# A hybrid encoder layer on one core: the short convolution in token order, and RWKV's output weights and merge operands by pairs of columns

## The chip, the cores and the metric

The kernel runs on one core of one Trainium2 chip. The metric is the device time of one execution in microseconds (us); the median over several runs is compared. The engines of a core are named PE (matrix multiply, with PEld for its weight loads), DVE (vector), ACT (scalar and activation), POOL and SP (which here issues the DMA transfers). Each works through its own list of instructions in a fixed order and waits at an instruction until what it needs is there.

## The reference

One layer of an encoder, for 1024 tokens of 1024 channels in float32:

```python
x = x + 0.5 * swiglu(rmsnorm(x, ffn1_norm), ffn1_w_gu, ffn1_w_down)
h = rmsnorm(x, mix_norm)
u_hy, u_rw, g_hy, g_rw = split(h @ w_in)          # 1536, 1952, 1024, 1024 columns
uc = w[0] * u_hy[t-1] + w[1] * u_hy[t] + w[2] * u_hy[t+1] + b    # centred width-3 conv
x1, x2, v = split(uc)                             # 512 channels each
z = x1 * long_conv(v, k_f[:, 0]); z = x2 * long_conv(z, k_f[:, 1])
y_hy = z @ hy_out
y_rw = rwkv7_two_scans(u_rw) @ rw_out             # 512 -> 1024 columns
merged = sigmoid(g_hy) * y_hy + sigmoid(g_rw) * y_rw
x = x + merged @ w_out
x = x + 0.5 * swiglu(rmsnorm(x, ffn2_norm), ffn2_w_gu, ffn2_w_down)
out = rmsnorm(x, final_norm)
```

The filters of the long convolution are made in the kernel from positions, by a small network. The time mixing of RWKV is a linear recurrence over the tokens, forward and backward, followed by a group norm, a bonus term and a gate.

## The kernel before

The activations lie transposed, channels on the 128 partitions and tokens along the free dimension. Nearly every large product is made of three products of 128x512 in a reduced float32: a factor is split into a high part and a rest, and hi x hi, lo x hi and hi x lo are summed in PSUM (`mm3`, lines 43 to 45; with the order pinned by `InOrder`, line 55). The split of weights is a cast on ACT (line 33) and a subtraction on DVE or POOL (line 37); `col_weights` loads 128 columns of a weight matrix to `w_st` (line 170, two buffers) and splits them to `w_hi` and `w_lo` (three buffers each).

The stages follow one another: first feed-forward, mixer input, RWKV's scan with other work filled in between, mixer output, second feed-forward. A scheduler lays out the order of each engine before the run, by priority in program order and by its own estimates of when buffers and operands are ready; on the chip the order is then fixed. Instructions that went through `InOrder` keep their order on PE.

Two places matter here.

**Short convolution** (`ShortConv`, within `mixer_in`). Twelve column groups of 128 channels pass through it. Each half of 512 tokens comes from PE in PSUM (`pw`). `take` copies it to `sh_u` (line 545) and writes the middle tap with its bias to `sh_o` (line 546). `finish` adds the two outer taps, each in one DVE pass over 1024 tokens (line 552), transposes eight blocks of 128x128 on PE (line 558, with `sh_o` as the stationary operand and the identity as the moving one), copies the result out on ACT (line 559) and stores it to `d_X` (line 560). Tokens are numbered t = 8 m + r. The long convolution wants, for each r, a block of 128 tokens m by channels. Before, `sh_o` has the shape (r, m): writes to it go in steps of 128 elements, and each transposed block is packed. In the same stage run the filters of the long convolution (lines 420 to 525), on PE, ACT, DVE and POOL.

**Mixer output** (`mixer_out`). The last RWKV blocks still need `RwkvPost`, the norm and gate: a unit `rest` already begun, and two units of blocks 0 and 7 whose operands (`rp_k`, `rp_r`, `rp_y`, `rp_v`, `rp_g`, `rp_gd`) `post.load` fetches. Their results go to `d_yo`, and the second half of the tokens is fetched from there (`z_st`, split to `s_hi` and `s_lo` by `split_half`). Meanwhile the first half can be multiplied with `rw_out`: for each half t and each of eight column groups j, twelve matmuls to `mo_ps` (four PSUM buffers), then on DVE the gate times the product (line 1605), plus Hyena's part (line 1606), and the split to `m_hi` and `m_lo`. The gate `mo_sg` and Hyena's part `mo_mh` are fetched by pairs of column groups, two buffers each (line 1583); the weights by single groups. After both halves comes the product with `w_out`.

## Time and profile before

| | |
|---|---|
| median of 3 runs | 2882.93 us (2874.61 to 2890.05) |
| profiled execution | 2875.99 us, span of its instructions 2874.2 us, mean granted PE clock 0.97 |
| PE busy | 2723.9 us (95%), weight loads 2194.6 us beside it |
| DVE, ACT, POOL busy | 1231.8, 905.2, 550.0 us |
| moved by DMA | 276.43 MB, 96 GB/s in the mean |
| short convolution with filters | from 790 to 1066 us of the span |
| RWKV's output weights | from 1932.8 to 2017.4 us |

The span runs from the first to the last instruction of the profiled execution; its time is a little longer. A page shows how long each engine was busy, then its busy share in 40 slices. A view of waits names for each engine's instruction what released it, and for how long the engine had been idle ahead of it: total, number, longest. A timeline row has start, length, engine, line, operation and, in brackets, the idle time before it and its releaser. A row of a tile gives the shortest, the median and the longest duration in nanoseconds.

### The profile page before, as it was taken

To read this page: it belongs to the slowest core of one execution; us is meant where nothing else is said; L and a number is where in the kernel's file an instruction comes from. 1 tells how busy PE (TensorE), PEld (TensorE's weight loads), DVE (VectorE), ACT (ScalarE), POOL (GpSimd) and SP (SyncE) were. 2 spreads that over 40 slices of the span, in tenths; PEclk is the share of its full clock that TensorE was granted. 3 is DMA by queue.
4 is the path that set the end of the run, shared out by engine and by line. 5 is a ranking of instruction groups with operands and counts; after the bars stand their busy time and mean duration, and the time that the engine had idled before them with its cause. 6 is when DMAs were issued, how large, how long until landed. Compare 5 with 4: busy or idle time off the path is not lost. (4 is left out here: it accounts for less than half of the span.)

```text
span 2874.2 us, 46016 instructions
## 1 busy us (share of the span) xinstructions
PE 2723.9 (95%) x19440; PEld 2194.6 (76%) x19440; DVE 1231.8 (43%) x2140; ACT 905.2 (31%) x1515; POOL 550.0 (19%) x351
## 2 busy tenths in 40 slices
PE   8999999999988899989899999898999999999998
PEld 6888888888665667777787877776778888888787
DVE  4111010111647668998765667757541111101114
ACT  5111111111444442334654545532331111111112
POOL 2323233232413210000000000000033232322322
PEclk9999999999988999999999999898999999999999
DMA  5111111111341235553644325457531111111102
GB/s 126 55 48 48 41 55 48 41 52 43 107 148 63 77 127 186 164 169 114 188 118 152 103 88 180 144 171 231 166 88 52 44 52 44 52 44 48 47 27 92
DMA packets 406477, 276.43 MB, mean 96 GB/s; under 512 B 50899, under 2 KB 366879, under 8 KB 405632
## 3 DMA queue, kind: packets, MB, share of 16 engines
q1 hardware_dynamic: 406272, 273.50, 31.5%
q8 instruction: 153, 2.51, 0.4%
q14 instruction: 52, 0.43, 0.0%
HBM read 202.53 MB, written 70.91 MB: 95 GB/s over the span
## 5 line engine op out<-in xcount | busy, mean ns | idle before, releaser
L45 PE MATMUL pw<-hThi,w_lo 128*128 128x512 f32 (+1 forms) x1184 | 472.3, 400 | 15.6 <-DVE w_lo L1246 15.6
L43 PE MATMUL pw<-hThi,w_hi 128*128 128x512 f32 (+1 forms) x1184 | 473.8, 400 | 8.5 <-ACT sh_o L1268 4.4
L44 PE MATMUL pw<-hTlo,w_hi 128*128 128x512 f32 (+1 forms) x1184 | 472.1, 399 | 0.0
L33 ACT CAST w_hi<-w_st 128x1024 fp32r<-128x1024 f32 (+1 forms) x176 | 170.8, 972 | 496.0 <-PE pw L44 187.0
L37 POOL TENSOR_TENSOR w_lo<-w_st,w_hi 128x1024 fp32r<-128x1024 f32 x100 | 240.5, 2405 | 412.3 <-ACT w_hi L33 406.1
L43 PE MATMUL pgu<-hThi,w_hi 128*128 128x512 f32 x704 | 279.0, 396 | 0.8 <-issue 0.8
L44 PE MATMUL pgu<-hTlo,w_hi 128*128 128x512 f32 x704 | 279.1, 396 | 0.2 <-POOL hTlo L37 0.2
L45 PE MATMUL pgu<-hThi,w_lo 128*128 128x512 f32 x704 | 279.1, 397 | 0.0
L43 PE MATMUL pdn<-g_hi,wd_hi 128*128 128x512 f32 x704 | 275.0, 391 | 1.9 <-DVE xT L226 1.9
L44 PE MATMUL pdn<-g_lo,wd_hi 128*128 128x512 f32 x704 | 274.8, 390 | 2.0 <-POOL g_lo L37 2.0
L45 PE MATMUL pdn<-g_hi,wd_lo 128*128 128x512 f32 x704 | 275.0, 391 | 1.4 <-POOL wd_lo L37 1.4
L45 PEld LDWEIGHTS pw<-hThi,w_lo 128*128 128x128 f32 (+1 forms) x1184 | 223.2, 189 | 69.6 <-DVE w_lo L1246 17.8
L43 PEld LDWEIGHTS pw<-hThi,w_hi 128*128 128x128 f32 (+1 forms) x1184 | 223.6, 189 | 63.9 <-ACT sh_o L1268 6.2
L226 DVE SCALAR_TENSOR_TENSOR xT<-pdn,xT 128x512 f32<-128x512 f32 x192 | 132.3, 690 | 314.8 <-PE pdn L45 314.8
L44 PEld LDWEIGHTS pw<-hTlo,w_hi 128*128 128x128 f32 (+1 forms) x1184 | 223.3, 189 | 54.6 <-issue 4.4
L209 DVE TENSOR_TENSOR silu<-silu,pgu 128x512 f32<-128x512 f32 x44 | 30.2, 687 | 449.5 <-PE pgu L45 449.5
L209 DVE TENSOR_TENSOR silu<-silu,pw 128x512 f32<-128x512 f32 x44 | 30.2, 687 | 445.9 <-PE pw L45 445.1
L37 POOL TENSOR_TENSOR wd_lo<-wdst,wd_hi 128x512 fp32r<-128x512 f32 (+1 forms) x112 | 132.4, 1183 | 333.6 <-ACT wd_hi L33 333.6
L37 POOL TENSOR_TENSOR g_lo<-silu,g_hi 128x512 fp32r<-128x512 f32 x88 | 113.5, 1289 | 398.4 <-ACT g_hi L33 398.4
L33 ACT CAST wd_hi<-wdst 128x512 fp32r<-128x512 f32 (+1 forms) x112 | 64.5, 576 | 379.5 <-PE pdn L44 366.9
L37 POOL TENSOR_TENSOR hTlo<-nm_h,hThi 128x512 fp32r<-128x512 f32 x16 | 23.2, 1447 | 740.2 <-ACT hThi L33 740.2
L43 PEld LDWEIGHTS pgu<-hThi,w_hi 128*128 128x128 f32 x704 | 132.5, 188 | 33.2 <-issue 1.2
(316 smaller groups left out, 4461.6 us busy)
## 6 DMA issues: line engine op xcount, KB each, us to landing
w_st<-in_ffn_w_gu SPq DMA_DIRECT2D x88, 512.0 KB, 3.7
w_st<-in_w_in SPq DMA_DIRECT2D x57, 512.0 KB, 3.8
wdst<-in_ffn_w_down SPq DMA_DIRECT2D x64, 256.0 KB, 2.8
wdst<-in_ffn_w_down SPq DMA_DIRECT2D x48, 192.0 KB, 2.5
d_kf<-kout SPq DMA_DIRECT2D x32, 256.0 KB, 2.3
hy_k<-d_kf SPq DMA_DIRECT2D x32, 256.0 KB, 3.3
w_st<-in_w_out SPq DMA_DIRECT2D x16, 512.0 KB, 3.9
d_X<-sh_x SPq DMA_DIRECT2D x12, 512.0 KB, 3.5
```

The lines of the kernel that those rows point to most:

```text
L33: nc.scalar.copy(hi, src)
L37: eng.tensor_tensor(lo, src, hi.bitcast(F32), ALU.subtract)
L43: te.matmul(out, lhs[0], rhs[0], start=first, stop=False)
L44: te.matmul(out, lhs[0], rhs[1], start=False, stop=False)
L45: te.matmul(out, lhs[1], rhs[0], start=False, stop=last)
L209: nc.vector.tensor_tensor(sl, sl, pu, ALU.mult)
L226: nc.vector.scalar_tensor_tensor(xa, ps, 0.5, xa, ALU.mult, ALU.add)
```

## The change

Short convolution: `sh_o` keeps the tokens in order. The middle tap and the two outer taps are written in one packed run. The transposes then take every eighth column as their stationary operand. No instruction is added, removed or moved in this stage; what moves, lies in the operands' steps.

Output weights: `weights` loads 256 columns (512 rows of 1 KB instead of two times 512 rows of 512 B), splits 128x1024 elements at once, and uses the whole of the `w_st`, `w_hi` and `w_lo` buffers where half was used. Gates and Hyena's part of a pair are fetched by one transfer each in the first half and two each in the second, where two and two were. `ahead(n)` issues the weights and gates of pair n, one pair before they are used; pair 0 comes ahead of the post units, pair 1 behind them in the program.

```diff
         self.uc = pool.tile([P, L], F32, name="sh_o", tag="sh_o")
-        nc.scalar.activation(self.ucv[:, ts(t, 64), :], ps.rearrange("p (m r) -> p m r", r=RT),
-                             AF.Identity, bias=cw[:, 3:4], scale=cw[:, 1:2])
+        nc.scalar.activation(self.uc[:, ts(t, 512)], ps, AF.Identity, bias=cw[:, 3:4], scale=cw[:, 1:2])
...
-            nc.vector.scalar_tensor_tensor(ucv, u[:, j : j + L].rearrange("p (m r) -> p m r", r=RT),
-                                           cw[:, j : j + 1], ucv, ALU.mult, ALU.add)
+            nc.vector.scalar_tensor_tensor(uc, u[:, j : j + L], cw[:, j : j + 1], uc, ALU.mult, ALU.add)
...
-                nc.tensor.transpose(pt[:, q], uc[:, 4 * h + q, :], self.ident)
+                nc.tensor.transpose(pt[:, q], uc[:, 4 * h + q :: RT], self.ident)
...
-            weights = lambda j: col_weights(nc, wp, I["rw_out"][:, ts(j, P)], 4, lo_eng="dve")
-            w = [weights(0), weights(1)]
+            def weights(i):
+                st, hi, lo = [wp.tile([P, KD, P], dt, name=n, tag=n, bufs=b) for n, dt, b in
+                              (("w_st", F32, 2), ("w_hi", F32R, 3), ("w_lo", F32R, 3))]
+                nc.sync.dma_start(st.rearrange("p (k c) f -> p k (c f)", c=2),
+                                  I["rw_out"][:, ts(i, 2 * P)].rearrange("(k p) f -> p k f", p=P))
+                split_from(nc, hi, lo, st, "act", "dve")
+                return [x.rearrange("p (k c) f -> p k c f", c=2) for x in (hi, lo)]
...
-                    for j in range(2):
-                        a = dr[n][ts(2 * i + j, P)].rearrange("p (h t) -> p h t", t=256)
-                        nc.sync.dma_start(x[:, j].rearrange("p (h t) -> p h t", t=256), a[:, 1:3] if t == 0 else a[:, 0::3])
+                    a = dr[n][ts(i, 2 * P)].rearrange("(j p) (h t) -> p j h t", p=P, t=256)
+                    if t == 0:
+                        nc.sync.dma_start(x, a[:, :, 1:3].rearrange("p j h t -> p j (h t)"))
+                    else:
+                        for h in range(2):
+                            nc.sync.dma_start(x[:, :, ts(h, 256)], a[:, :, 3 * h])
...
-            gates(0, 0)
+            def ahead(n):
+                if n < 2 * KD // 2:
+                    w.append(weights(n % 4))
+                    gates(n // 4, n % 4)
+            w = []
+            ahead(0)
...
             y = [y0]
+            ahead(1)
...
-                    if j % 2 == 0 and (t, j // 2) not in merge:
-                        gates(t, j // 2)
+                    if j % 2 == 0 and t + j:
+                        ahead(4 * t + j // 2 + 1)
...
-                    wj = w.pop(0) if w else weights(j)
+                    if j % 2 == 0:
+                        w2 = w.pop(0)
+                    wj = [x[:, :, j % 2] for x in w2]
```

How the laid-out order moves at three places. First SP's transfers at the end of RWKV's scan, ahead of the last units' loads (`w_st` is a weight load, `d_y` the scan's last result), before:

```order
L1497 DMA rp_k_17549<-d_kd_88 128x2x256
L1554 DMA d_yo<-rp_y_17116 128x2x256
L1137 DMA d_y_86<-rw_y 128x512
L1137 DMA d_y_87<-rw_y 128x512
L170 DMA w_st<-in_rw_out 128x4x128
L1497 DMA rp_y_17547<-d_y_86 128x2x256
L170 DMA w_st<-in_rw_out 128x4x128
L1583 DMA mo_sg<-d_sg 128x512 x2
L1583 DMA mo_mh<-d_mh 128x512 x2
L1497 DMA rp_k_17671<-d_kd_88 128x2x512
```

and in the changed kernel:

```order
L1494 DMA rp_k_17549<-d_kd_88 128x2x256
L1574 DMA w_st<-in_rw_out 128x4x256
L1551 DMA d_yo<-rp_y_17116 128x2x256
L1134 DMA d_y_86<-rw_y 128x512
L1134 DMA d_y_87<-rw_y 128x512
L1574 DMA w_st<-in_rw_out 128x4x256
L1494 DMA rp_y_17547<-d_y_86 128x2x256
L1588 DMA mo_sg<-d_sg 128x2x512
L1588 DMA mo_mh<-d_mh 128x2x512
L1494 DMA rp_k_17663<-d_kd_88 128x2x512
```

Two more weight loads stand ahead of these rows in both. Before, four single column groups are asked for ahead of the last units' operands, now four pairs; the third stands ahead of `d_yo` and `d_y` instead of behind them.

Second, DVE at the same time, behind the last state update of the scan (`w_lo` is a subtraction of weights, lines 1545 to 1552 are the end of a post unit), before:

```order
L1548 TENSOR_TENSOR rp_y_17116<-rp_y_17116,psA 128x512
L37 TENSOR_TENSOR w_lo<-w_st,w_hi 128x512
L1550 TENSOR_SCALAR rp_y_17116<-rp_y_17116,k_post 128x2x128 x2
L37 TENSOR_TENSOR w_lo<-w_st,w_hi 128x512
L1551 TENSOR_TENSOR rp_y_17116<-rp_y_17116,rp_k_17118 128x512
L1552 TENSOR_TENSOR rp_y_17116<-rp_y_17116,psA 128x512
L1520 TENSOR_TENSOR rp_k_17549<-rp_k_17549,rp_k_17550 128x256 x2
```

and in the changed kernel:

```order
L1545 TENSOR_TENSOR rp_y_17116<-rp_y_17116,psA 128x512
L1547 TENSOR_SCALAR rp_y_17116<-rp_y_17116,k_post 128x2x128 x2
L37 TENSOR_TENSOR w_lo<-w_st,w_hi 128x1024
L1548 TENSOR_TENSOR rp_y_17116<-rp_y_17116,rp_k_17118 128x512
L37 TENSOR_TENSOR w_lo<-w_st,w_hi 128x1024
L1549 TENSOR_TENSOR rp_y_17116<-rp_y_17116,psA 128x512
L1517 TENSOR_TENSOR rp_k_17549<-rp_k_17549,rp_k_17550 128x256 x2
```

The second subtraction, now of a pair, stands between the unit's last two steps.

Third, DVE at the end of the last post unit, whose result the second half of the tokens waits for, before:

```order
L1551 TENSOR_TENSOR rp_y_17669<-rp_y_17669,rp_k_17671 128x2x256
L840 COPY rp_k_17672<-hr_r 128x2x256
L1552 TENSOR_TENSOR rp_y_17669<-rp_y_17669,psA 128x2x256
L37 TENSOR_TENSOR w_lo<-w_st,w_hi 128x512
L1548 TENSOR_TENSOR rp_y_17669<-rp_y_17669,psA 128x2x256
L1550 TENSOR_SCALAR rp_y_17669<-rp_y_17669,k_post 128x2x128 x2
L1551 TENSOR_TENSOR rp_y_17669<-rp_y_17669,rp_k_17671 128x2x256
L1552 TENSOR_TENSOR rp_y_17669<-rp_y_17669,psA 128x2x256
```

and in the changed kernel (lines 1623 and 1624 are the merge, 1605 and 1606 before):

```order
L1548 TENSOR_TENSOR rp_y_17661<-rp_y_17661,rp_k_17663 128x2x256
L1624 TENSOR_TENSOR mo_sg<-mo_sg,mo_mh 128x512
L1549 TENSOR_TENSOR rp_y_17661<-rp_y_17661,psA 128x2x256
L1545 TENSOR_TENSOR rp_y_17661<-rp_y_17661,psA 128x2x256
L37 TENSOR_TENSOR m_lo<-mo_sg,m_hi 128x512
L1547 TENSOR_SCALAR rp_y_17661<-rp_y_17661,k_post 128x2x128 x2
L1623 SCALAR_TENSOR_TENSOR mo_sg<-mo_sg,mo_ps 128x512
L1548 TENSOR_TENSOR rp_y_17661<-rp_y_17661,rp_k_17663 128x2x256
L1624 TENSOR_TENSOR mo_sg<-mo_sg,mo_mh 128x512
L1549 TENSOR_TENSOR rp_y_17661<-rp_y_17661,psA 128x2x256
```

Steps of the merge stand among those of the unit where one subtraction of weights stood. On PE, six column groups of the first half now come ahead of the two units' first matmuls, where four did.

More of the change, by code (lines that the diff above doesn't have):

```diff
@@ L539, in __init__ @@
         nc.vector.memset(u[:, L + 1 : L + 2], 0.0)
-        self.uc = pool.tile([P, RT, P], F32, name="sh_o", tag="sh_o")
-        self.ucv = self.uc.rearrange("p r m -> p m r")
+        self.uc = pool.tile([P, L], F32, name="sh_o", tag="sh_o")
     def take(self, t, ps):
@@ L545, in take @@
         nc.scalar.copy(self.u[:, 1 + 512 * t : 513 + 512 * t], ps)
-        nc.scalar.activation(self.ucv[:, ts(t, 64), :], ps.rearrange("p (m r) -> p m r", r=RT),
-                             AF.Identity, bias=cw[:, 3:4], scale=cw[:, 1:2])
+        nc.scalar.activation(self.uc[:, ts(t, 512)], ps, AF.Identity, bias=cw[:, 3:4], scale=cw[:, 1:2])
     def finish(self, dst):
-        nc, u, uc, ucv, cw = self.nc, self.u, self.uc, self.ucv, self.cw
+        nc, u, uc, cw = self.nc, self.u, self.uc, self.cw
         for j in (0, 2):
-            nc.vector.scalar_tensor_tensor(ucv, u[:, j : j + L].rearrange("p (m r) -> p m r", r=RT),
-                                           cw[:, j : j + 1], ucv, ALU.mult, ALU.add)
+            nc.vector.scalar_tensor_tensor(uc, u[:, j : j + L], cw[:, j : j + 1], uc, ALU.mult, ALU.add)
         o = self.xpool.tile([P, RT, P], F32, name="sh_x", tag="sh_x")
```

## The prediction

> **What bounds the kernel now.** I read the page from the top: which engine is full, then where it is not.
>
> ```profile
> PE 2723.9 (95%) x19440; PEld 2194.6 (76%) x19440; DVE 1231.8 (43%) x2140; ACT 905.2 (31%) x1515; POOL 550.0 (19%) x351
> ...
> PEclk9999999999988999999999999898999999999999
> ```
>
> TensorE is busy for 95% of the span and no other engine for half of it, so an edit counts where it takes time from PE or lets PE wait less. PE's clock digit (40 slices of 71.9 us, counted from 0) is 8 in slices 11, 12, 25 and 27. 11 and 12 are the start of the short convolution, 27 is the stage of RWKV's output weights: the two places edited. Busy time by stretches of both (first number: length; then busy time of each engine; then PE's granted clock, DMA share, GB/s):
>
> ```profile
> core 0: us, PE busy (x) PEld busy (x) DVE busy (x) ACT busy (x) POOL busy (x), PEclk, DMA share, GB/s
> 790.00:1066.00 276.00, 239.41 (x948) 175.04 (x949) 178.59 (x312) 132.02 (x191) 64.45 (x38) 0.93 0.30 97
> ...
> 1990.00:2017.40 27.40, 24.73 (x96) 19.27 (x96) 17.76 (x29) 8.92 (x15) 0.00 (x0) 0.92 0.74 211
> 1932.80:2017.40 84.60, 71.15 (x276) 50.31 (x276) 59.75 (x117) 22.92 (x39) 0.00 (x0) 0.90 0.75 236
> ```
>
> PE idles 36.6 us of 276 in the convolution stage and 13.5 us of 84.6 in the output-weight stage. A clock of 0.93 over 276 us is worth up to 19 us, 0.90 over 84.6 us up to 8.5 us. These four numbers cap what the change can win. Who PE waits for in the first stage:
>
> ```profile
> PE hy_tp L558 <- DVE sh_o L552: 17.3, 10, 3.6
> PE ps_h L501 <- DVE ac L499: 6.9, 4, 4.4
> PE pw L43 <- ACT sh_o L546: 3.9, 1, 3.9
> PE hy_tp L558 <- DVE sh_u L539: 3.6, 1, 3.6
> PE hy_tp L558 <- issue: 2.6, 1, 2.6
> ```
>
> Twelve convolutions, twelve waits of the transposes L558, 23.5 us in total: PE reaches them in its fixed order before the convolution is ready.
>
> **Short conv, step by step.** The rows of the tile sh_o (duration min/median/max) hold both the old forms and, from RWKV's token shift, the new ones:
>
> ```profile
> L558 PEld LDWEIGHTS hy_tp<-ident,sh_o x96: 137/142/232, 806.9 to 1065.4; 128*128 128x128 f32 x96
> L558 PE MATMUL hy_tp<-ident,sh_o x96: 272/273/476, 806.9 to 1065.5; 128*128 128x128 f32 x96
> L1268 ACT ACTIVATE sh_o<-pw,k_mu x32: 669/692/700, 1063.2 to 1327.4; 128x512 f32<-128x512 f32 x30, 32x512 f32<-32x512 f32 x2
> L1281 DVE SCALAR_TENSOR_TENSOR sh_o<-sh_u,k_mu,sh_o x32: 1267/1277/1285, 1072.8 to 1341.7; 128x1024 f32<-128x1024 f32 x30, 32x1024 f32<-32x1024 f32 x2
> L546 ACT ACTIVATE sh_o<-pw,k_cw x24: 1202/1261/1312, 790.0 to 1058.3; 128x512 f32<-128x512 f32 x24
> L552 DVE SCALAR_TENSOR_TENSOR sh_o<-sh_u,k_cw,sh_o x24: 1945/2008/3925, 802.1 to 1062.6; 128x1024 f32<-128x1024 f32 x24
> ```
>
> L546 becomes L1268's form but for a bias: 1261 to 692 ns, 0.57 us each. L552 becomes L1281's: 2008 to 1277 ns, 0.73 us each. All 24 of each save 14 us of ACT and 18 us of DVE, which are idle half the stage and count for nothing by themselves. What counts is the chain ahead of one group of transposes, here the seventh:
>
> ```profile
> 941.87 1.28 ACT L546 ACTIVATE sh_o<-pw,k_cw 128x512 f32<-128x512 f32 x1
> 943.18 2.08 DVE L552 SCALAR_TENSOR_TENSOR sh_o<-sh_u,k_cw,sh_o 128x1024 f32<-128x1024 f32 x1 [1.04 <-ACT sh_o L546]
> 946.37 1.95 DVE L552 SCALAR_TENSOR_TENSOR sh_o<-sh_u,k_cw,sh_o 128x1024 f32<-128x1024 f32 x1
> 948.47 1.07 PE L558 MATMUL hy_tp<-ident,sh_o 128*128 128x128 f32 x8 [2.28 <-DVE sh_o L552]
> 818.42 1.94 PE L558 MATMUL hy_tp<-ident,sh_o 128*128 128x128 f32 x8 [3.55 <-DVE sh_u L539]
> ```
>
> ACT, two DVE passes, PE: the chain gets shorter by 2 x 0.73 = 1.46 us, and by 0.57 more where DVE itself waited for ACT, 2.03 us. A wait can give back at most itself. The three long ones (3.6, 3.6, 2.6) give about 2 us each and keep 3.7; the other nine total 13.7, 1.5 each, and go nearly whole. I take 19 of 23.5. The first wait of the stage (3.9, PSUM of two conv takes) gives 0.6. The other waits of the list stay. No engine's order of instructions moves in this stage.
>
> The clock: behind the long waits PE runs slowly, as the last row shows against the one above it: 1.94 instead of 1.07 us for the same eight transposes. If three or four such spells vanish they give up to 8 us (1.5 to 2.6 each, from 0.9 us of transposes and as much of matmuls behind them); some may stay, I take 5. The Trainium skill (TensorE: Matmul & The Clock Gate, What's actually happening) says that a window of about 3.4 us of idleness halves the clock and a busy one restores it. By that rule the waits of 3.6, cut to 1.6, would cost no spell at all, and the term would be nearer 8 than 5.
>
> What is added: the transposes now load as weights every eighth column of sh_o, 32 bytes apart, which no TensorE row here does. Below: nothing, 142 ns stays. Above: the nearest 32-byte step of another engine is ACT's write L766 against a packed copy of the same 256 elements L1133 (mean ns behind the bar):
>
> ```profile
> L1133 ACT COPY rw_y<-psY 128x256 f32<-128x256 f32 x16 | 5.9, 368 | 24.5 <-PE psY L55 24.5
> L766 ACT COPY hy_zT<-hy_t 128x256 f32<-128x256 f32 x16 | 9.1, 686 | 4.7 <-PE hy_t L764 4.7
> ```
>
> 318 ns more for 256 elements, 1.24 ns each, so 159 ns for 128 columns and 15.3 us for 96 loads. Between them stands DVE's L552, the only row that also reads in steps: 731 ns for 1024 elements, 91 ns for 128. I take that one, as a read is in question: 96 x 91 ns = 8.7 us on PE, since the eight loads follow each other at about 110 ns (1.07 us for eight) with nothing to hide behind. The Trainium skill (Advanced Engine Details and Errata, SBUF Cachelines) speaks against the change here: an access that leaves its 16-byte line each time pays, and two hits on a line are needed for full rate. With a rate halved by it, the estimate is some 107 ns a load, 10 us in all; had a packed rate held, none.
>
> Sum of the short conv: 19 + 0.6 + 5 - 8.7 = 16 us won. I take off 2, because a part of what PE gains here will meet the filters' own chain (L499 to L501) earlier: 14, between 2 (no clock, the load at 15.3) and 28 (the load free, the clock at 8).
>
> **Output weights of RWKV, step by step.** The waits of PE, with the loads and DVE steps around them:
>
> ```profile
> 1932.85 0.48 PE L43 MATMUL mo_ps<-s_hi,w_hi 128*128 128x512 f32 x1 [0.31 <-DVE rp_y L1552]
> 1940.06 0.50 PE L43 MATMUL mo_ps<-s_hi,w_hi 128*128 128x512 f32 x1 [1.36 <-ACT w_hi L33]
> 1952.74 1.23 PE L1526 MATMUL psA<-rp_y,rp_ones 128*128 128x512 f32 x2 [3.78 <-DVE rp_y L1523]
> 1990.09 0.79 PE L43 MATMUL mo_ps<-s_hi,w_hi 128*128 128x512 f32 x1 [4.49 <-ACT w_hi L33]
> 2017.49 0.50 PE L43 MATMUL mo_ps<-m_hi,w_hi 128*128 128x512 f32 x1 [2.01 <-ACT w_hi L33]
> 2018.98 0.79 PE L43 MATMUL mo_ps<-m_hi,w_hi 128*128 128x512 f32 x1 [0.76 <-ACT w_hi L33]
> ```
>
> ```profile
> 1934.66 0.72 SPq L170 DMA_DIRECT2D w_st<-in_rw_out  x1
> 1955.96 1.02 SPq L170 DMA_DIRECT2D w_st<-in_rw_out  x2
> 1979.70 0.36 SPq L1596 DMA_DIRECT2D z_st<-d_yo  x1
> 1985.12 2.74 SPq L170 DMA_DIRECT2D w_st<-in_rw_out  x2
> ```
>
> ```profile
> 1930.63 0.69 DVE L37 TENSOR_TENSOR w_lo<-w_st,w_hi 128x512 fp32r<-128x512 f32 x1
> 1932.02 0.69 DVE L1552 TENSOR_TENSOR rp_y<-rp_y,psA 128x512 f32<-128x512 f32 x1
> 1986.24 1.22 DVE L37 TENSOR_TENSOR s_lo<-z_st,s_hi 128x1024 fp32r<-128x1024 f32 x1
> 2017.47 1.23 DVE L37 TENSOR_TENSOR w_lo<-w_st,w_hi 128x1024 fp32r<-128x1024 f32 x1 [1.42 <-ACT w_hi L33]
> ```
>
> Now four pairs of weights, 2 MB, go out on SP ahead of the last post unit's loads, where four columns (1 MB) did. The 1.36 us wait for the third column goes. The start gets later: two 1.23 us subtractions stand ahead of L1552 where two of 0.69 stood, and the loads are twice as large; PE starts about 1.2 us later. Queued behind are that unit's d_yo and the loads of the next; the extra MB at the stage's 236 to 315 GB/s is 3 to 4 us, part of it before DMA is full, so L1523 comes about 1.3 us later. PE no longer idles for it: columns five and six, 24 matmuls, fill the 3.78 us. But that only moves the stall. The second half of the tokens needs the chain unit, d_yo, z_st, s_lo (ready 1986.24 + 1.22 = 1987.5), and on DVE four merges now stand among the last unit's steps where one subtraction stood, 2 us more against 1.7 us less of slow clock. What I do gain there: the weights of the second half are in hand (before, loads issued at 1985.12 made PE wait until 1990.09), 1990.1 - 1987.5 = 2.6 us, from 0 to 4.5. The pair ahead also takes about half of 2.0 + 0.8 at the entry to w_out and the small weight waits before it, 1.7, and the clock (0.92 over 27.4 us, worth 2.2) about 0.7. Sum: 5 us won (1.36 and 1.2 cancel), from -3 to 12. Wider casts and fewer DMA issues (1 instead of 2 per gate tile at first) lie beside PE's work and count nothing; should DVE become the bound (60 of 84.6 us now) they would count 2 us.
>
> **Sum.** 14 + 5 = 19 us. The profiled execution took 2876.0 us (span 2874.2), the median of the three runs is 2882.9, 0.24% above it. 2876 - 19 = 2857 for a profiled execution, 2864 for the median.
>
> **Rivals.** *Packed rate*: the stepped load costs PE nothing and the clock recovers; 28 + 5 = 33 us, 2850. For it: no PE row shows a slow load. Against: both stepped rows of other engines are slow. Chance 0.15. *The wait moves on*: PE, 2 us earlier at each transpose, waits as much longer for the filters (the L499 row, POOL's accumulations behind it); a third of 24.6 is left, less half the load's price, plus the output weights: 8 - 4 + 5 = 9, 2874. For it: DVE is 65% busy and PE's order is fixed. Against: waits other than the transposes and the first one sum to under 10 us. Chance 0.20. *Output weights lose*: the second half comes later by DVE's merges; 14 - 3 = 11, 2872. Chance 0.05. *Slower*: the stepped load, at L558's place, takes four times 142 ns, +426 ns x 96 = 41 us, against 30 won: 2894. It decides from 30 us / 96 = 0.31 us more per load, some 3.2 times the packed one; the other engines' rows show 1.6 to 1.9 times. Chance 0.05. The forecast itself, 0.55, spans 2856 to 2873.
>
> Half a per cent, 14.4 us, is about what a measurement of this kernel can tell from no change. Faster by more: 0.15 + 0.47 of the forecast's 0.55 = 0.62. Within: 0.08 + 0.20 + 0.05 = 0.33. Slower: 0.05. Range 2848 to 2880: it leaves out half of the packed rival above 33 us won and, at the other end, the slower one.
>
> **What would show it.** Rows of the changed kernel: the conv's DVE pass at 1277 ns and its ACT pass at 692; LDWEIGHTS of hy_tp at 142 (packed), 233 (my price) or above 450 ns (slower); waits of hy_tp on DVE 4 to 5 us in place of 23.5; fewer slow spells between 800 and 970. In the output stage: no PE wait at L1523's place, one before the second half that ends by 1988, less than 2 us at the entry to w_out. I am wrong if the waits stay while the passes get shorter, or if eight transposes take over 3 us.

## The result and the profile after

| | before | changed |
|---|---|---|
| median | 2882.46 us of 4 runs (2874.61 to 2890.05) | 2847.31 us of 4 runs (2846.73 to 2848.61) |
| the same beside a later group of kernels | 2882.38 us of 11 runs (2874.18 to 2889.16) | 2849.49 us of 5 runs (2843.13 to 2853.17) |
| ratio, 95% interval | | 0.9883 [0.9865, 0.9901]; later 0.9884 [0.9864, 0.9904] |
| span of the profiled execution | 2874.2 us | 2845.6 us |

The changed kernel is faster by 35 us in the first comparison and by 33 in the second. The prediction had 19 (2864, range 2848 to 2880). The sign and the places were right, the size was little more than half, and the measured median lies 0.7 us below the range's lower end, the later one 1.5 us above it.

The page of the changed kernel, busy time of PE and its clock in 40 slices:

```profile
PE 2715.7 (95%) x19440; PEld 2189.7 (77%) x19440; DVE 1215.3 (43%) x2132; ACT 893.4 (31%) x1507; POOL 546.7 (19%) x351
...
PEclk9999999999999999999999999898999999999999
```

The two slices of the short convolution that showed an 8 (11 and 12) now show a 9. Both edited stages by windows (length; busy time of PE, PEld, DVE, ACT, POOL; clock, DMA share, GB/s), the second window cut from the last matmul of the scan to the first of w_out:

```profile
core 0: us, PE busy (x) PEld busy (x) DVE busy (x) ACT busy (x) POOL busy (x), PEclk, DMA share, GB/s
791.00:1040.50 249.50, 231.60 (x949) 169.64 (x950) 162.69 (x310) 121.36 (x191) 61.03 (x38) 0.97 0.33 107
1910.90:1990.20 79.30, 70.07 (x289) 50.88 (x283) 60.57 (x113) 22.32 (x33) 0.00 (x0) 0.89 0.76 248
```

The output window cut in the same way was 85.3 us before (from 1932.20 to 2017.49 us), so it is 6.0 us shorter. The convolution stage takes 249.5 us where it took 276.0, with the same number of matmuls but one: 26.5 us less. Of these, idle time of PE fell from 36.6 to 17.9 us, 18.7 less, and its busy time from 239.4 to 231.6, 7.8 less at equal work, with the granted clock up from 0.93 to 0.97. PE's waits there:

```profile
PE ps_h L501 <- DVE ac L499: 6.9, 4, 4.3
...
PE pw L43 <- ACT sh_o L545: 3.4, 1, 3.4
...
PE hy_tp L555 <- DVE sh_o L550: 2.7, 2, 2.4
...
PE hy_tp L555 <- DVE sh_u L539: 1.9, 1, 1.9
...
PE hy_tp L555 <- issue: 1.2, 1, 1.2
```

Twelve waits of the transposes with 23.5 us became four with 5.8. The filters' wait (L501) is what it was, 6.9. The tile's rows with the new forms:

```profile
L555 PEld LDWEIGHTS hy_tp<-ident,sh_o x96: 186/193/208, 805.0 to 1039.6; 128*128 128x128 f32 x96
L555 PE MATMUL hy_tp<-ident,sh_o x96: 270/276/377, 805.1 to 1039.8; 128*128 128x128 f32 x96
...
L545 ACT ACTIVATE sh_o<-pw,k_cw x24: 758/782/811, 791.0 to 1034.0; 128x512 f32<-128x512 f32 x24
L550 DVE SCALAR_TENSOR_TENSOR sh_o<-sh_u,k_cw,sh_o x24: 1271/1279/3265, 801.2 to 1037.5; 128x1024 f32<-128x1024 f32 x24
```

DVE's pass came out as forecast (1279 against 1277 ns), ACT's took 782 and not 692, and the stepped weight load 193 ns where the packed one took 142.

The waits in the stage of the output weights, and behind it the first in w_out:

```profile
1913.38 0.47 PE L43 MATMUL mo_ps<-s_hi,w_hi 128*128 128x512 f32 x1 [2.17 <-DVE rp_y L1549]
1922.17 1.10 PE L55 MATMUL psA<-rp_y,rp_ones 128*128 128x512 f32 x2 [0.40 <-DVE rp_y L1520]
1960.23 1.22 PE L43 MATMUL mo_ps<-s_hi,w_hi 128*128 128x512 f32 x2 [3.82 <-ACT s_hi L33]
1963.37 0.80 PE L44 MATMUL mo_ps<-s_lo,w_hi 128*128 128x512 f32 x1 [1.92 <-DVE s_lo L37]
1968.88 1.22 PE L43 MATMUL mo_ps<-s_hi,w_hi 128*128 128x512 f32 x2 [0.88 <-ACT s_hi L33]
...
2014.75 0.50 PE L43 MATMUL mo_ps<-m_hi,w_hi 128*128 128x512 f32 x1 [2.63 <-ACT w_hi L33]
2016.01 0.50 PE L45 MATMUL mo_ps<-m_hi,w_lo 128*128 128x512 f32 x1 [0.53 <-DVE w_lo L37]
```

No wait for weights is left in rw_out. The waits of the second half now name its operand (s_hi, s_lo): the product starts before the operand is whole. Before, the last two rows had forerunners with 0.75 and 0.53 at the same place:

```profile
2042.68 0.51 PE L43 MATMUL mo_ps<-m_hi,w_hi 128*128 128x512 f32 x1 [0.75 <-ACT w_hi L33]
2043.94 0.51 PE L45 MATMUL mo_ps<-m_hi,w_lo 128*128 128x512 f32 x1 [0.53 <-DVE w_lo L37]
```

### The profile page after: what moved, and what is told of

It is laid out like the page before. It is cut to its first block, busy times and chain, and to the rows that moved or that the text cites. A ratio compares the mean times of both kernels' runs of the same rounds, so it can differ in the third digit from the quotient of the medians.

```text
span 2845.6 us, 45944 instructions
## 1 busy us (share of the span) xinstructions
PE 2715.7 (95%) x19440; PEld 2189.7 (77%) x19440; DVE 1215.3 (43%) x2132; ACT 893.4 (31%) x1507; POOL 546.7 (19%) x351
## 5 line engine op out<-in xcount | busy, mean ns | idle before, releaser
L45 PEld LDWEIGHTS pw<-hThi,w_lo 128*128 128x128 f32 (+1 forms) x1184 | 222.3, 188 | 69.3 <-DVE w_lo L1243 17.7
```

What stands on the lines that cost most here:

```text
L45: te.matmul(out, lhs[1], rhs[0], start=False, stop=last)
```

## The experiments

One measure goes through all of them. Every kernel here has the same 19440 matmuls on PE, so a stage is measured from the start of one matmul, counted from the first, to that of another, whatever the time ahead of it did. "Conv" is from the 3401st (where the windows above begin) to the 4351st, "scan" from there to the 15496th, whose source is the same in all kernels, "output" from there to the 16101st, which lies four fifths into w_out. In us, worked out from the starts in each trace:

| kernel | conv | scan | output | median |
|---|---|---|---|---|
| before | 275.2 | 865.6 | 161.9 | 2882 |
| short convolution alone | 250.6 | 874.0 | 164.5 | 2861.6 |
| output weights alone | 273.6 | 870.6 | 152.6 | 2871.5 |
| changed | 249.0 | 870.1 | 155.3 | 2847.3 |
| changed, later group | 250.4 | 869.8 | 156.6 | 2849.5 |
| pairs, but not ahead | 250.3 | 865.4 | 155.9 | 2853.6 |
| all three passes in steps | 284.4 | 870.7 | 153.8 | 2881.2 |
| ACT's pass in steps | 254.1 | 868.8 | 156.8 | 2852.5 |
| packed load | 248.4 | 873.0 | 154.8 | 2849.1 |
| fetch ahead of gates | 249.1 | 866.7 | 150.0 | 2846.6 |
| two groups of w_out early | 249.1 | 870.3 | 160.6 | 2853.4 |

Conv repeats within 2 us wherever its code is the same. Output repeats less well: 161.9 and 164.5 us with the old code, 152.6 to 156.8 in the six kernels with pairs one ahead and the transfers in their order. The scan differs by up to 8.6 us between executions. Most kernels have one profile, so a difference of a few us in output or scan is not read as the edit's.

**The two parts, each alone.** One kernel has the new `ShortConv` and the old `mixer_out`, the other the reverse (the hunks of the diff are those shown ahead of the prediction).

> Only the short convolution in token order; RWKV's output weights as before. Theory: the two parts add up and the convolution is the larger. The trace of the changed kernel has PE 26 us further ahead at the end of this stage than at its start (from 0.5 behind to 25.7 ahead), so I expect 26 us less than before, 2856 where before has 2882, and hy_tp's waits at about 6 us. Rival: of these 26 us, some 4 are given back in RWKV's scan, whose code is unchanged (25.7 ahead at 1041 us, 21.3 at 1911): if that comes from the edit and not from the one execution, the gain is 22 and this trace gives the 4 back at the same places.

> Only the output weights, gates and Hyena's part by pairs, one pair ahead; the short convolution as before. Theory: PE gained 8.5 us between the start of the stage and the last of the second half in the changed kernel's trace and lost 2 in the weights of w_out behind it, so 6 to 7 us less than before, 2876. The prediction's own number for it was 5. Rival: the gain needs the shift by 20 us in the scan ahead of it (other transfers in flight), and this part alone gives under 3 us. A second thing is read here: the convolution stage is the same as before, so its waits of hy_tp, 23.5 us in the trace of before, show how much they vary from one execution to the next; and if the times spread as before's do (2874 to 2890) while those without the old convolution don't, the spread lies in it.

Measured: the convolution alone 2861.64 us of 6 runs (2854.51 to 2866.86) against 2881.67 of 23 (2873.81 to 2890.87), ratio 0.9926 [0.9907, 0.9946], or 16 to 27 us won. The output weights alone 2871.54 of 12 runs (2861.59 to 2879.39), ratio 0.9961 [0.9947, 0.9976], or 7 to 15 us. The parts add up: 0.9926 x 0.9961 = 0.9887, the whole is 0.9883. In the stages, conv falls from 274.4 (mean of 275.2 and 273.6) to 249.7 (mean of six), 24.7 us (the six: the convolution alone, the two rows of the changed kernel, and the three whose edit lies in the output stage only); output from 163.2 (mean of 161.9 and 164.5) to 155.0 (mean of the six kernels with pairs one ahead and the transfers in their order), 8.2 us. Together 32.9 us, close to the 33 and 35 us by times.

The rival on the scan falls. The convolution alone did spend 8 us more in the scan than before, but the kernel "pairs, but not ahead" has the same convolution and spends 865.4, as before did. What one profile takes away there another gives back, so it belongs to the execution. This also answers the second point of the second expectation: the old convolution stage repeats (275.2 and 273.6), and the kernels without it spread too, by 12 us in six runs (the convolution alone) and 15 in six (pairs, but not ahead, below), where before has 17 in 23. The changed kernel's own first four runs lay within 2 us by chance:

> The changed kernel once more, beside the others. Its first four times lay within 2 us (2846.7 to 2848.6), those of before and of the three variants so far within 13 to 17. Theory: the spread comes from RWKV's scan, whose parts differ by 4 to 6 us between the profiles of kernels with the same code there (65.1 against 59.5 us for the last thousand matmuls but five hundred), so the changed kernel has it too: 2840 to 2858, median 2848 to 2852. Rival: the short convolution's long waits made the spread, and the times stay within 3 us.

Its five later runs are from 2843.13 to 2853.17, as expected. That the scan makes the spread is argued from the table, where it varies most, and not shown run by run. Comparing one profile of before (2876.0, at the low end of its range) with one of the changed kernel would have given 28.6 us instead of 33 to 35.

**The stepped load by itself.**

```diff
-                nc.tensor.transpose(pt[:, q], uc[:, 4 * h + q :: RT], self.ident)
+                nc.tensor.transpose(pt[:, q], uc[:, ts(4 * h + q, P)], self.ident)
```

> The changed kernel, but the transposes load 128 neighbouring columns of the tile and not every eighth; the tokens then lie in another order within the long convolution's input, so that its result is another one, and the work is the same. It measures the stepped load by itself. The prediction priced it at 91 ns a load, 8.7 us in all. Theory now: the traces show 193 ns instead of 142 for a load, but the eight transposes follow each other every 122 ns instead of every 113, so 96 x 9 ns = 0.9 us, and the time is that of the changed kernel within 2 us. Rival (the prediction's): 8 to 9 us faster than the changed kernel.

Measured: 2849.11 us of 5 runs, ratio 0.9884 [0.9864, 0.9905], the same as the changed kernel beside it (2849.49). The row of its loads, and the fourth group of eight transposes in the changed kernel and in this one (start, length):

```profile
L555 PEld LDWEIGHTS hy_tp<-ident,sh_o x96: 138/141/143, 804.5 to 1038.5; 128*128 128x128 f32 x96
```

```profile
836.58 1.13 PE L555 MATMUL hy_tp<-ident,sh_o 128*128 128x128 f32 x8
```

```profile
835.85 1.06 PE L555 MATMUL hy_tp<-ident,sh_o 128*128 128x128 f32 x8
```

The load is 52 ns longer in steps (193 against 141), but eight transposes take 1.13 instead of 1.06 us, 9 ns each: four fifths of the load's extra length lie beside the matmuls. In the stage that is 12 x 0.07 = 0.8 us; the two conv stages differ by 0.6 to 2.0. By times the difference is too small to be told. The rival's 8 to 9 us are excluded by the stage; the two intervals alone would barely exclude them.

**The chain's length.** The tile stays in token order and the stepped load stays too, but the passes run through the tile in steps of eight:

```diff
-            nc.vector.scalar_tensor_tensor(uc, u[:, j : j + L], cw[:, j : j + 1], uc, ALU.mult, ALU.add)
+            ucr = uc.rearrange("p (m r) -> p r m", r=RT)
+            nc.vector.scalar_tensor_tensor(ucr, u[:, j : j + L].rearrange("p (m r) -> p r m", r=RT),
+                                           cw[:, j : j + 1], ucr, ALU.mult, ALU.add)
```

and ACT's likewise; then ACT's alone.

> The changed kernel with the tile still in token order and the transposes still loading every eighth column, but the three passes that write it go through it in steps of eight elements again (same result). It puts the chain's length back and keeps everything else, the stepped load above all. Theory: the passes' length is what PE waited for; with about 0.7 us more a DVE pass and 0.5 an ACT pass the waits of hy_tp come back to 20 us or more and the clock's slow spells with them: 24 to 28 us slower than the changed kernel, 2871 to 2875. Rival: the change of the tile's layout did it otherwise (the transposes' operand itself), and the time stays below 2855 although the passes are long.

> The changed kernel, but ACT's pass (middle tap and bias) goes through the packed tile in steps of eight elements; DVE's two passes stay packed. In the kernel with all three passes in steps ACT's took 1304 ns instead of 782, DVE's 2178 instead of 1279, and the stage got 34 to 35 us longer: 12 convolutions with 2 x 0.90 + 2 x 0.52 = 2.84 us each are 34. Theory: PE waits for the whole chain, microsecond for microsecond, so this alone costs 12 x 0.52 to 12 x 1.04 = 6 to 12 us in the stage (256 to 262 us instead of 249 to 250), 2856 to 2861. Rival: with short DVE passes most of the waits are gone and ACT's extra half microsecond hides in what is left: under 3 us.

Measured: all three passes 2881.24 us of 10 runs, ratio to before 1.0000 [0.9986, 1.0015], 32 to 34 us slower than the changed kernel, more than the 24 to 28 expected. ACT's alone 2852.52 of 6 runs, ratio 0.9898 [0.9878, 0.9918], 3 to 5 us slower than the changed kernel by the medians, whose intervals overlap. The passes of the first, then of the second:

```profile
L545 ACT ACTIVATE sh_o<-pw,k_cw x24: 1239/1304/1444, 790.1 to 1067.0; 128x512 f32<-128x512 f32 x24
L552 DVE SCALAR_TENSOR_TENSOR sh_o<-sh_u,k_cw,sh_o x24: 2030/2178/3983, 802.1 to 1071.7; 128x1024 f32<-128x1024 f32 x24
```

```profile
L545 ACT ACTIVATE sh_o<-pw,k_cw x24: 1242/1322/1423, 789.9 to 1038.5; 128x512 f32<-128x512 f32 x24
L551 DVE SCALAR_TENSOR_TENSOR sh_o<-sh_u,k_cw,sh_o x24: 1270/1278/3248, 801.1 to 1042.0; 128x1024 f32<-128x1024 f32 x24
```

These passes were slower than the old ones (2178 against 2008 ns), which is one reason why the first expectation was too small. With the length of the chain (one ACT pass and two DVE passes) against that of the stage the readings fall in line:

| kernel | chain, us | 12 x chain above the changed one | conv stage above it |
|---|---|---|---|
| changed | 0.78 + 2 x 1.28 = 3.34 | 0 | 0 (249.7) |
| ACT's pass in steps | 1.32 + 2 x 1.28 = 3.88 | 6.5 | 4.4 |
| before | 1.26 + 2 x 2.01 = 5.28 | 23.3 | 24.7 |
| all passes in steps | 1.30 + 2 x 2.18 = 5.66 | 27.8 | 34.7 |

The stage grows with the chain, but not by one mechanism. PE's idle time in the stage is 17.5 us in the mean of the changed convolution; it grows by 2.0, 18.1 and 23.7 us in the three rows below it, always less than the chain. The rest, 2.4, 6.6 and 11.0 us, is PE's busy time at equal work, which the slow clock stretches: the records of the granted clock have 17 us at half speed in the changed kernel's stage, 41 in before's and 44 with all passes in steps. That the sum comes so near the chain's length for before is in part luck. ACT's 0.54 us a convolution costs 4.4 of 6.5 us in the stage: below the lower end of what was expected (6), above the rival's 3. Since all of the loss came back with the passes in steps while the layout stayed, no gain is left for the tile's layout as such.

**Pairs without the step ahead.**

```diff
-            ahead(1)
-                        ahead(4 * t + j // 2 + 1)
+                        ahead(4 * t + j // 2)
```

> The changed kernel, with pairs of columns, but each pair's weights and gates asked for where they are first used and no longer one pair ahead (pair 0 still ahead of the post units). Theory: the gain of this part lies in the weights of the second half and of w_out being in hand; without it PE waits again for w_hi at the start of the second half and behind it, 5 us more than the changed kernel, 2852. Rival: the width alone does it (half the transfers, half the casts): the same time as the changed kernel, 2847, within 1.5 us.

Measured: 2853.56 us of 6 runs (2844.27 to 2859.09), ratio 0.9893 [0.9872, 0.9914]. By the medians 4 to 6 us slower than the changed kernel, but its scatter of 15 us covers that. The output stage of its one profile, from the fastest of its six runs, is 155.9 us, as long as the changed kernel's (155.3 and 156.6). So the theory's 5 us are not seen in the stage, and the rival, that the width of the pairs gives the gain, fits better; with the scatter of this stage, a step ahead that is worth a few us is not excluded. Whether it is the width of the weights or that of the gates was not separated. What does change is where PE waits. Here all waits of the second half are one:

```profile
1966.30 0.79 PE L43 MATMUL mo_ps<-s_hi,w_hi 128*128 128x512 f32 x1 [13.79 <-ACT w_hi L33]
```

PE waits 13.8 us for the weights and then works without a stop to the end of the stage. One pair ahead, it starts 10 us earlier, counted from the last matmul of the scan, on a first part of the operand, and loses as much again by waits and slow clock.

**The fetch of the second half ahead of its gates.** The store and the fetch of the last unit's result, in the changed kernel (SP's queue, then the cast that waits for it):

```profile
1958.07 0.36 SPq L1551 DMA_DIRECT2D d_yo<-rp_y  x1
...
1961.86 0.36 SPq L1612 DMA_DIRECT2D z_st<-d_yo  x1
```

```profile
1967.79 1.04 ACT L33 CAST s_hi<-z_st 128x1024 fp32r<-128x1024 f32 x1 [4.96 <-DMA z_st<-d_yo]
```

From store to cast 9.7 us. The experiment binds the order of these transfers on SP and asks for the second half's first gates behind the fetch:

```diff
-                            nc.sync.dma_start(x[:, :, ts(h, 256)], a[:, :, 3 * h])
+                            tc.keep_in_program_order(nc.sync.dma_start(x[:, :, ts(h, 256)], a[:, :, 3 * h]))
...
-                    gates(n // 4, n % 4)
+                    if n != 4:
+                        gates(n // 4, n % 4)
...
-                    y.append(split_half(nc, wp, yb, lambda st, h: nc.sync.dma_start(st, ...)))
+                    y.append(split_half(nc, wp, yb, lambda st, h: tc.keep_in_program_order(nc.sync.dma_start(st, ...))))
+                    gates(1, 0)
```

> The changed kernel, but on the queue of transfers the fetch of the second half of the tokens (z_st) stands ahead of the second half's gates, and those of its first pair are asked for behind it. In the changed kernel's trace the second fetch is issued 3.8 us after the store it reads (2.1 us for the first) and takes 5.9 us, while five gate transfers and a pair of weights go out around it. Theory: these delay it; without them s_lo is ready 4 us earlier, and PE, which idles 6.6 us and runs slowly for 10 us there, wins 3 to 5 us: 2844 where the changed kernel has 2848. Rival: the gates then come late for the merges and the weights behind them, and nothing is won.

Measured: 2846.56 us of 5 runs (2839.26 to 2850.26), ratio 0.9880 [0.9858, 0.9901]; not to be told from the changed kernel by times. In the trace:

```profile
1955.35 0.36 SPq L1551 DMA_DIRECT2D d_yo<-rp_y  x1
1957.52 0.36 SPq L1613 DMA_DIRECT2D z_st<-d_yo  x1
```

```profile
1961.20 1.04 ACT L33 CAST s_hi<-z_st 128x1024 fp32r<-128x1024 f32 x1 [1.09 <-DMA z_st<-d_yo]
```

From store to cast 5.9 us, 3.9 less, as expected. The output stage is 150.0 us, 5 to 7 less than in the changed kernel's two profiles, and only part of it at this place: the waits of 2.63 and 0.53 us in w_out are gone too. The three kernels further below that keep this order have 149.4 to 149.9 us there, and no kernel without it is below 152.6, so this gain is seen in the stage in four profiles, though not in the times.

**Columns of w_out ahead of the second half.** The first half's merge is nearly done when PE waits for the second half, so w_out's first groups could be multiplied there:

```diff
+                    early_ps = [product(j, 0) for j in range(NEARLY)]
                     y.append(split_half(...))
...
-                ps = pm.tile([P, 512], F32, name="mo_ps", tag="mo_ps")
...
+                ps = early_ps[j] if t == 0 and j < NEARLY else product(j, t)
```

> The changed kernel, but the first two column groups of w_out for the first half of the tokens are multiplied before the second half of rw_out (48 matmuls, 11 us) and wait in two of the four PSUM buffers. The first half's merge is all they need. Theory: in the changed kernel's trace PE has nothing left while the last post unit's result goes out and comes back: 3.8 + 1.9 + 0.9 us idle and some 27 matmuls at 430 instead of 230 ns, 12 us; the 48 matmuls fill it, and 8 to 12 us are won, 2838. Rival: their weights, 1 MB, go over the same queue as the second half's fetch, and two PSUM buffers are too few for the second half: within 3 us of the changed kernel.

Measured, two groups ahead: 2853.38 us of 6 runs, ratio 0.9904 [0.9884, 0.9924], no gain; its output stage is 160.6 us. Two waits took the place of the old ones, for the rest of the early weights and for the addition to xT:

```profile
1965.56 0.80 PE L46 MATMUL mo_ps<-m_hi,w_lo 128*128 128x512 f32 x1 [6.50 <-DVE w_lo L38]
...
2017.80 0.77 PE L44 MATMUL mo_ps<-m_hi,w_hi 128*128 128x512 f32 x1 [5.52 <-DVE xT L1643]
```

The rival was right on the result. Its reason, transfers and PSUM, is at most part of it: PE waits first for a subtraction on DVE. Two further kernels look at it below.

**Taps by halves.** What is left of the chain can be cut from the other side. The outer taps of the first 512 tokens need only the first take, except that the last of these tokens has its next neighbour in the second; that one is left to the second half:

```diff
+        for j, a, b in ((0, 0, 512), (2, 0, 511)) if t == 0 else ((0, 512, L), (2, 511, L)):
+            nc.vector.scalar_tensor_tensor(self.uc[:, a:b], self.u[:, a + j : b + j], cw[:, j : j + 1],
+                                           self.uc[:, a:b], ALU.mult, ALU.add)
...
-        for j in (0, 2):
-            nc.vector.scalar_tensor_tensor(uc, u[:, j : j + L], cw[:, j : j + 1], uc, ALU.mult, ALU.add)
```

> The kernel with the second half's fetch ahead of its gates (profile 2837.5, median 2846.6), and the short convolution's two outer taps added by halves: the first half of the tokens when it has been taken, so that behind the second half's take two passes of 512 stand where two of 1024 did, 2 x 0.68 instead of 2 x 1.28 us. Theory: the chain gets 1.2 us shorter a convolution, and what is left of the transposes' waits, 5 to 6 us with one slow spell, goes: 4 to 7 us faster than without, 2840 to 2842. Rival: the twelve waits are gone as far as they can be, the rest of the idle time (17 us in this stage) waits for the filters and for PSUM, and 24 more DVE instructions delay the filters' chain: no change or slower.

> As the one before, and one column group of w_out for the first half of the tokens (24 matmuls, 5.5 us) ahead of the second half, where two groups brought a wait of 6.5 us for their weights and one of 5.5 behind. Theory: the weights of one group fit into the free time of the queue ahead of the last post unit, so its 24 matmuls fill the 3.7 us in which PE waits for the second half and keep part of its clock: 3 to 6 us faster than the kernel before it. Rival: the weights of the second half and of w_out are then late by one group, as with two: no gain.

> The kernel before it (taps by halves, fetch ahead of the gates, one column group of w_out ahead of the second half), but the rest of that column's weights (w_lo) is subtracted on POOL, which does nothing in this stage, and not on DVE. In the trace with DVE the weights' cast is done at 1942 us of the span, the subtraction stands behind the last post unit and starts at 1952.6, and PE waits 6.5 us for it. Theory: the fill failed by that place in DVE's order and by nothing else; with POOL the wait goes, the 24 matmuls stand in the time in which PE waited 3.8 us for the second half, and the stage is 4 to 6 us shorter than without the fill: 2826 to 2828 where the kernel without it has 2831. Rival: the transfers set the second half's time in any case (two stores, then two fetches, then gates and weights on one queue), and PE waits behind the 24 matmuls for what it waited for ahead of them: 2830 to 2836.

Measured: taps by halves 2831.46 us of 5 runs (2826.56 to 2840.05) against 2882.98, ratio 0.9830 [0.9806, 0.9853]; with one early group of w_out 2836.18 of 5 (2832.43 to 2838.69), ratio 0.9841 [0.9818, 0.9864]; with its rest of the weights on POOL 2828.82 of 5 (2822.00 to 2836.47), ratio 0.9819 [0.9790, 0.9849]. The intervals of the first and the third lie below the changed kernel's; among the three there is no difference that these runs can tell. The taps, in the kernel without early groups, and PE's waits:

```profile
L547 DVE SCALAR_TENSOR_TENSOR sh_o<-sh_u,k_cw,sh_o x48: 734/742/2851, 791.4 to 1033.5; 128x512 f32<-128x512 f32 x24, 128x511 f32<-128x511 f32 x12, 128x513 f32<-128x513 f32 x12
```

```profile
PE ps_h L501 <- DVE ac L499: 4.9, 4, 2.7
...
PE hy_tp L556 <- DVE sh_o L547: 1.6, 2, 0.9
...
PE hy_tp L556 <- issue: 1.1, 1, 1.1
...
PE hy_tp L556 <- DVE sh_u L539: 0.2, 1, 0.2
```

The transposes' waits fall from 5.8 to 2.9 us and the filters' from 6.9 to 4.9. As PE's order shifts a little at the end of the stage, it is read over a longer stretch, from the 3401st to the 7001st matmul: 652.9 to 656.9 us in the six profiles with the changed convolution, 644.6, 643.4 and 646.3 in the three with the halves. That is 10 us, more than expected; the other 5 of the 15 us between the medians (2846.6, 2831.5) lie within their scatter. On the early groups the rival holds both times: the output stage is 149.6 us without, 149.4 with one, 149.9 with one and POOL. With one early group PE again waits 6.5 us for w_lo. On POOL that wait is gone and PE works ahead as meant, and the time goes into smaller waits, of which these are the largest two between the last post unit and the second half:

```profile
1957.60 0.50 PE L44 MATMUL mo_ps<-m_hi,w_hi 128*128 128x512 f32 x1 [1.72 <-ACT m_hi L34]
...
1960.76 0.79 PE L45 MATMUL mo_ps<-m_lo,w_hi 128*128 128x512 f32 x1 [0.85 <-DVE m_lo L38]
```

The early group needs the last columns of the merge, which DVE and ACT finish only now. What bounds the stage there was not settled further.

## Why the prediction was right or wrong

Short conv, forecast 14 us, measured 24.7:

- *The waits, 19 + 0.6, less 2 for the filters.* Right. PE's idle time in the stage fell by 18.7 us; 17.7 of them are the transposes' waits (23.5 to 5.8), 0.5 the first wait (3.9 to 3.4). "A wait can give back at most itself" held for each; the three long ones gave 1.2 to 1.7 us and not 2 each, and kept 1.2, 1.9 and 2.4 us. The 2 us for the filters' chain were not lost: L501 has 6.9 us before and after. The rival "the wait moves on" falls with it.
- *The stepped load, 8.7.* This step failed. It measured 0.8 us. Two parts of it were wrong: the price of the load itself (52 ns, not 91, which was DVE's row), and that there was "nothing to hide behind": of the 52 ns only 9 lengthen the rhythm of the transposes. The Trainium skill (Advanced Engine Details and Errata, SBUF Cachelines) names a penalty for such an access, but neither an engine nor a size. The 107 ns a load and 10 us were an estimate with a rate halved; the load's row shows the direction, at half that size, and the loss of time is not there.
- *The clock, 5, at most 8.* Mis-sized. PE's busy time fell by 7.8 us at equal work, with the load's 0.8 already against it, so the clock gave 8.6. In the means of two and of six profiles the stage lost 24.7 us, of which 18.1 idle (35.6 to 17.5); the clock is then about 7. So the term came nearer to 8 than to 5, but not because short waits cost nothing: waits of 1.94 and 2.41 us were still followed by slow clock (last section).
- In sum, of the 11 us that were missing 8 come from the load and 2 to 3.6 from the clock; the filters kept their 2 and the waits gave 1 less than thought.

Output weights, forecast 5 us, measured 8.2 in the stage:

- *The start later by 1.2.* It was 1.9 later (a wait of 2.17 for 0.31 us), for the reason named: two subtractions of 1.22 us ahead of the unit's last step.
- *The 1.36 and the 3.78 us waits go.* Right; 0.40 us is left ahead of the post units.
- *The stall only moves on, and the second half starts 2.6 us earlier.* Half right. Counted from the last matmul of the scan it started 8.5 us earlier (after 49.4 us against 57.9), because the weights are in hand and PE begins with the first part of the operand. But of these 8.5 us 6 were lost again by s_lo, by the second fetch and by slow clock until 1973 us. The operand itself was whole later: its last s_lo ended after 59.2 us, and after 55.3 before. Nothing in the prediction had the fetch itself become slower, 9.7 us from store to cast. Before, it took 5.9:

```profile
1977.51 0.36 SPq L1554 DMA_DIRECT2D d_yo<-rp_y  x1
```

```profile
1983.38 1.05 ACT L33 CAST s_hi<-z_st 128x1024 fp32r<-128x1024 f32 x1 [0.80 <-DMA z_st<-d_yo]
```

  The step ahead is not what slows it, since without it the same way takes 9.6 us; with the fetch ahead of the second half's gates it takes 5.9.
- *Entry to w_out, 1.7.* The waits of 2.01 and 0.76 us went whole, and the next ones grew from 0.75 + 0.53 to 2.63 + 0.53: 0.9 net.
- *The clock, 0.7.* None: 0.89 over the stage, after 0.90.
- The five terms do not each meet their number, and the sum is within its range (-3 to 12). That the gain was due to the weights being in hand one pair earlier is not borne out; the pairs alone have the same stage in their one profile. Which step of the output part gives the 8 us stays open.

The step from profile to median, 0.24% added, was wrong as well. Before's profiled execution lay at the low end of its kernel's times (its scan took 865.6 us), the changed kernel's in the middle (870.1). The rival "packed rate" had the time, 2850, and nearly its mechanism (the load almost free, the clock back); 0.15 was too low a chance for it. Against it I had set the rows of ACT and DVE, whose prices did not carry over to PE's loads. The two rivals that lost time are out: the output weights alone gain, although their second half did come later, and a load is 1.4 times the packed one, far from the 3.2 from which it would have turned the sign.

## What to carry to other kernels

Where an engine that is full waits in fixed order for a short chain on engines that are mostly idle, the stage pays for most of the chain's length, and for the slow clock behind the waits, and the step of an operand belongs on the side where the access is hidden: here the stepped access cost 0.73 us a pass on DVE (0.90 in steps of 32 bytes) and 9 ns a transpose on PE. Price such an access by the same engine's rows or not at all: keep both bounds, and don't put the middle on another engine's rate. Compare stages between the same two instructions of each trace; a single pair of spans carried 4 to 9 us of scatter from a stage that nobody had touched.

## What the runs showed of the hardware

The slow clock does not follow a wait's length alone. The second group of transposes in two kernels with the same convolution, the convolution alone and the later profile of the changed kernel:

```profile
812.48 1.78 PE L555 MATMUL hy_tp<-ident,sh_o 128*128 128x128 f32 x8 [1.94 <-DVE sh_u L539]
```

```profile
812.76 1.13 PE L555 MATMUL hy_tp<-ident,sh_o 128*128 128x128 f32 x8 [1.94 <-DVE sh_u L539]
```

And the eighth before the change, then with the output weights alone:

```profile
963.65 1.84 PE L558 MATMUL hy_tp<-ident,sh_o 128*128 128x128 f32 x8 [0.64 <-DVE sh_o L552]
```

```profile
964.32 1.07 PE L558 MATMUL hy_tp<-ident,sh_o 128*128 128x128 f32 x8 [0.64 <-DVE sh_o L552]
```

After the same wait the same eight transposes take 1.78 or 1.13 us, 1.84 or 1.07. What tells them apart is how the idle time falls on windows of 3.41 us. In the records of the granted clock, every slow spell of the convolution stage is one to four such windows long, and all of a trace lie on one grid, which lies otherwise in each execution. The windows around the first pair (start and end, length, PE's busy time and the others', clock):

```profile
809.35:812.77 3.42, 1.48 (x5) 0.51 (x5) 3.37 (x4) 0.78 (x1) 1.91 (x1) 1.00 0.60 163
812.77:816.18 3.41, 3.41 (x13) 2.95 (x12) 2.24 (x5) 1.17 (x2) 0.00 (x0) 0.50 0.50 142
```

```profile
808.05:811.47 3.42, 2.78 (x10) 1.31 (x8) 3.38 (x2) 1.43 (x2) 2.45 (x1) 1.00 0.94 257
811.47:814.88 3.41, 2.12 (x13) 1.94 (x14) 3.25 (x7) 1.30 (x3) 0.07 (x1) 1.00 0.57 156
```

In the first, the 1.94 us lie in one window, which is idle for 0.57 of its length, and the next is granted 0.50. In the second they are divided between two windows, idle for 0.19 and 0.38, and the clock stays. In the second pair another wait of 2 us lies just ahead of the one shown; before the change both fall mostly into one window (0.57 idle), with the output weights alone they are divided (0.45 and 0.32).

The same count over the convolution stage (785 to 1080 us of the span) of all fourteen profiles has 1123 windows at full clock. All 49 in which PE idled for 0.55 or more were followed by a slow one, 3 of the 4 between 0.52 and 0.55, and none of the 1070 below. Over the whole kernel all 207 windows idle for 0.6 or more were followed by a slow one, but so were 32 of 10471 idle for less than 0.3, so this share is not the whole rule. The Trainium skill (TensorE: Matmul & The Clock Gate, What's actually happening) says that the window of some 3.4 us over which idleness is judged runs freely, whatever the kernel does; these pairs agree with that. A wait of 1.9 us then costs a spell of slow clock or none, by where the windows happen to lie, and a shorter wait makes it rarer. That this is the cause was not tried by an experiment of its own.

A weight load in steps of 32 bytes was 52 ns longer than a packed one, and cost 9 ns a transpose in their rhythm.
